# A gate and up pass with its instructions left in written order, fewer GpSimd subtractions and a separate ring for side work

## The chip, the core and the metric

The kernel runs on one core of a Trainium2 chip. The metric is the device time of one execution, in microseconds (us). TensorE is called PE, VectorE DVE, ScalarE ACT, GpSimd POOL, and SyncE SP; here SP issues nearly every transfer.

## What is computed

One decoder layer on a sequence of 2048 rows of width 1024: a mixer of four head groups, an output projection with its residual, and a gated feed-forward block. Only the feed-forward block is touched:

```python
x = x + mixed @ w_out[l]
gu = rms_norm(x, norm_ffn[l]) @ w_gate_up[l]
x = x + (jax.nn.silu(gu[..., :D_FF]) * gu[..., D_FF:]) @ w_down[l]
```

D_FF is 2816, everything is float32.

## The kernel before

**Stages.** A and B compute the mixer, C the output projection, D the gate and up product with the silu, E the down product. Stages A, C, D and E are written as plain loops, and the tile framework's scheduler decides at compile time, by a priority in written order and its own clock, in which order each engine gets its instructions. Stage B (L795) opens a region called `manual_schedule` for all five engines, in which each engine gets the region's instructions in the order in which they are written.

**Precision.** A float32 product is made of three passes: each operand is split into a rounded high part and the low remainder, and PE adds high*high, low*high and high*low (L1589 to L1591). Splitting an operand is one ACT copy and one subtraction (`split`, L1528 to L1532, for weights; L1373 and L1374 for x).

**Stage D.** The work is cut as a 2 by 2 block product with seven block products instead of eight. A unit is one (b, s, a): b is the half of the rows (0, 1), s one of 11 sets of 256 columns (`NSET`), a is gate (0) or up (1). The order is b, then s, then a: 44 units. A unit has seven products of 12 matmuls (four slices of the contraction, three passes), each against one of seven fixed combinations of x: A11, S2, S1, S3, A12, A22, S4. For one half b, all seven x combinations stay in SBUF, split; they are loaded from `xf_d` (L1369 to L1374, 512 KB an instruction, two for each combination). When b goes from 0 to 1 they are loaded anew during the last unit of b = 0.

In `gate_up` (L1577 on) each product is followed by its eviction from the PSUM bank (L1598, L1602, L1606, L1610, L1614, L1615, L1618, L1621) and then by `step`, which writes one piece of the next unit's weight preparation (`prep_gu`) and one piece of side work. Three banks are used twice within a unit: p1, p7 and p5 get a second product added after their first eviction. So the product T4, the sixth, can't start before L1610 has read p7 after the fourth. After an up unit eight DVE operations (L1627 to L1634) form the seven combinations `hs` of the hidden values, and one transfer stores them (L1717).

**Preparation.** `prep_gu` forms four combinations of the raw weights on DVE (L1540, L1541, L1546, L1551), using a scratch tile `tt`, and splits seven operands. Six of the low parts are made by POOL and one (T4) by DVE (L1531). Raw weights come two units ahead into a ring `raw` of four 4 KB buffers (L1524).

**Side work.** Three kinds, all in b = 0: `prep_tw` forms differences of the down weights (four POOL subtractions a set, L1568 to L1573), in up units; `last_rows` finishes the last two row tiles of the x combinations (ACT, PE transposes at L1655, POOL, SP) in the gate units of s = 1 and 2; and x loads (L1369). Their buffers come from the same ring `raw` and from the same scratch `tt` (its tile for the down weights is `ttd`) as the weight preparation; `last_rows` shares the buffer of `hs`.

**Stage E** (L1818 to L1820 are its matmuls) loads `araw` (hidden) and `braw` (down weights), splits both and runs seven products.

Of the kernel before, what the change touches and what calls it, by code (L numbers as in the profile page):

```python
# [21 lines left out]
NT = T // 128  # L22
# [150 lines left out]
def kernel(ctx, tc, x, norm_mix, w_in, lru_conv_w, lru_conv_b, lru_w_gates, lru_b_gates,  # L173
# [1334 lines left out]
    with ExitStack() as Dx:  # L1508
        rw = Dx.enter_context(tc.tile_pool(name="rw", bufs=1, reuse_waits="tile"))
        gw = Dx.enter_context(tc.tile_pool(name="gw", bufs=10, reuse_waits="tile"))  # L1510
        xdb = Dx.enter_context(tc.tile_pool(name="xdb", bufs=1, reuse_waits="tile"))
        hp = Dx.enter_context(tc.tile_pool(name="hp", bufs=2, reuse_waits="tile"))
        psg = Dx.enter_context(tc.tile_pool(name="psg", bufs=7, space=PSUM, reuse_waits="tile"))
        pst = Dx.enter_context(tc.tile_pool(name="pst3", bufs=1, space=PSUM, reuse_waits="tile"))

        def raw_tile(name):
            return rw.tile([128, 1024], F32, name=name, tag="raw", bufs=4)

        def load_gu(s, a):
            c0 = a * DFF + s * 256  # L1520
            raws = []
            for c in range(2):
                raw = raw_tile("guraw").rearrange("p (k c) -> p k c", k=HK)
                SP.dma_start(raw, wgu[c * 512:(c + 1) * 512, c0:c0 + 256].rearrange("(k p) c -> p k c", p=128))  # L1524
                raws.append(raw)
            return raws

        def split(src, sub):  # L1528
            g = [gw.tile([128, HK, 128], F32R, name=f"g{a}") for a in "hl"]
            ACT.copy(g[0], src)  # L1530
            sub.tensor_sub(g[1], src, f(g[0]))  # L1531
            return g  # L1532

        def prep_gu(raws, ws):


            b11, b12, b21, b22 = raws[0][:, :, :128], raws[0][:, :, 128:], raws[1][:, :, :128], raws[1][:, :, 128:]
            tt = rw.tile([128, 2, HK, 128], F32, name="tt", tag="tt", bufs=1)
# [12 lines left out]
            DVE.tensor_sub(b21, b21, tt[:, 1])  # L1551
            yield
            ws["T4"] = split(b21, DVE)
            yield
            ws["B22"] = split(b22, POOL)
            yield

        def prep_tw(k):

            raws = []  # L1560
            for c in range(2):
                raw = raw_tile("dnraw")
                SP.dma_start(raw, wdn[(2 * k + c) * 128:(2 * k + c + 1) * 128, :])
                raws.append(raw)
            yield
            b11, b12, b21, b22 = [r[:, n * 512:(n + 1) * 512] for r in raws for n in range(2)]
            tt = rw.tile([128, 2, 512], F32, name="ttd", tag="tt", bufs=1)
            POOL.tensor_sub(tt[:, 0], b12, b11)  # L1568
            POOL.tensor_sub(tt[:, 1], b22, tt[:, 0])
            SP.dma_start(tw_d[k][0:2].rearrange("i p c -> p i c"), tt)  # L1570
            yield
            POOL.tensor_sub(b12, b22, b12)
            POOL.tensor_sub(b21, b21, tt[:, 1])  # L1573
            SP.dma_start(tw_d[k][2], b12)
            SP.dma_start(tw_d[k][3], b21)
            yield

        def gate_up(x, ws, gate, step):

# [16 lines left out]
            p1 = bank()  # L1596
            product(p1, "B11", A11, True)
            ACT.copy(ev[:, 0], p1)  # L1598
            step(A11)
# [3 lines left out]
            step(S2)  # L1603
            p5 = bank()
            product(p5, "T1", S1, True)
            ACT.copy(ev[:, 3], p5)  # L1606
            step(S1)
# [3 lines left out]
            step(S3)  # L1611
# [4 lines left out]
            step(A12)  # L1616
            product(p7, "T4", A22, False)
            DVE.tensor_add(ev[:, 2], p7, ev[:, 1])  # L1618
            step(A22)
            product(p5, "B22", S4, False)  # L1620
            DVE.tensor_add(ev[:, 1], p5, ev[:, 1])  # L1621
            if gate is None:
                ACT.activation(ev[:, 1:], ev[:, 1:], AF.Silu)
                step(S4)
                return ev
            hs = hp.tile([128, 7, 512], F32, name="hs", tag="hs", bufs=1)
            DVE.tensor_mul(hs[:, A11], p1, gate[:, 0])  # L1627
            DVE.tensor_mul(hs[:, A12], gate[:, 1], ev[:, 1])
            DVE.tensor_mul(gate[:, 2], gate[:, 2], ev[:, 2])
            DVE.tensor_mul(hs[:, A22], gate[:, 3], ev[:, 3])  # L1630
            DVE.tensor_add(hs[:, S1], gate[:, 2], hs[:, A22])
            DVE.tensor_sub(hs[:, S2], hs[:, S1], hs[:, A11])
            DVE.tensor_sub(hs[:, S3], hs[:, A11], gate[:, 2])
            DVE.tensor_sub(hs[:, S4], hs[:, A12], hs[:, S2])  # L1634
            step(S4)
            return hs

        def last_rows(t):

            buf = hp.tile([128, 3, 1024], F32, name="rows", tag="hs", bufs=1)  # L1640
            xt, xo, y = [buf[:, i] for i in range(3)]
# [8 lines left out]
            xo, y, s = [b.rearrange("p (k t) -> p k t", t=128) for b in (xo, y, xt)]  # L1650
# [8 lines left out]
            to_factors(t, xo, y, s, POOL)  # L1659
            yield  # L1660

        preps, side = [], []

        def run(todo):
            while todo:
# [12 lines left out]
        for q in seq[:2]:  # L1678
            raws[q] = load_gu(*q[1:])
        gu[seq[0]] = {}  # L1680
        preps.append(prep_gu(raws.pop(seq[0]), gu[seq[0]]))
        drain(preps)
        x = dict(x0)
        for i in LATE:
            x[i] = x_tiles(xdb, i)
            side.append(x_factor(0, i, x[i], rw, "raw", 4))
        run(side)
        new = {}
        for n, q in enumerate(seq):
            b, s, a = q  # L1690
            last = b == 0 and s == NSET - 1 and a == 1

            def step(i):
                run(preps)
                run(side)
                if n == 0:
                    run(side)
# [10 lines left out]
            if b == 0 and a == 0:  # L1708
                if s in (1, 2):
                    side.append(last_rows(NT - 3 + s))  # L1710
            if b == 0 and a == 1:
                side.append(prep_tw(s))
            if a == 0:
                gate = gate_up(x, gu.pop(q), None, step)
            else:
                hs = gate_up(x, gu.pop(q), gate, step)
                SP.dma_start(hf_d[b][s].rearrange("i p t -> p i t"), hs)  # L1717
            drain(preps)
            drain(side)
            if last:  # L1720
                x = new


    with ExitStack() as Ex:
# [11 lines left out]
        def total(i):  # L1736
            return lambda k: tw_d[k][i]

        prods = [(A11, block(0, 0)), (A12, block(1, 0)), (S2, total(1)), (S1, total(0)), (S4, block(1, 1)),
                 (S3, total(2)), (A22, total(3))]  # L1740
# [131 lines left out]
```

## Time and profile before

| | |
|---|---|
| median of 3 runs | 2805.86 us (2801.77 to 2811.09) |
| profiled execution | 2809.3 us |
| its span | 2807.5 us |
| mean granted TensorE clock | 0.977 of full |
| PE busy | 2640.9 us (94%) |
| DVE, ACT, POOL busy | 1731.3 (62%), 1343.1 (48%), 1122.7 us (40%) |
| transfers | 364.69 MB, 130 GB/s mean |

The span runs from the first to the last instruction of the profiled execution; 1.8 us of its time lie outside. Stage D stands at about 1413 to 2381 us of the span, with b = 0 until about 1929; stage E follows. A timeline row gives start, duration, engine, line, output and inputs, and in brackets the idle time before it and what ended that.

### The profile page before, as it was taken

The numbers are of one execution on the slowest core, as the hardware profiler recorded it, in microseconds if no ns is written. First come the engines' busy times: TensorE is split into PE (matmuls) and PEld (weight loads), VectorE is DVE, ScalarE is ACT, GpSimd is POOL, SyncE is SP. The second block draws the span as 40 slices with busy tenths as digits, with TensorE's granted clock in tenths as the row PEclk, the third lists the DMA queues.
The fourth block names the chain that finished last, engine by engine and source line by source line (L and its number), as shares of the span: only waits on it lengthen the run. The fifth ranks groups of instructions, "written<-read, shape, count | busy, mean of one in ns | idle before, by whom it ended". The sixth has DMA issues, their size and how long they took to land.

```text
span 2807.5 us, 39068 instructions
## 1 busy us (share of the span) xinstructions
PE 2640.9 (94%) x13483; PEld 2226.4 (79%) x13483; DVE 1731.3 (62%) x3701; ACT 1343.1 (48%) x2863; POOL 1122.7 (40%) x1118
## 2 busy tenths in 40 slices
PE   7999898999998999999978989897999999999999
PEld 6899767889888888988866767675788887888887
DVE  6762686358899999877665555455655654333343
ACT  5431574169988888875533222223333333433331
POOL 1100125124565568812055545453444443422450
PEclk9999999999999999999999999998999999999999
DMA  5444314253423110068656443345333332864563
GB/s 162 127 109 114 118 49 150 71 167 100 107 70 83 39 54 24 16 225 252 227 167 198 134 144 126 135 145 174 114 105 110 109 105 76 273 199 135 172 192 120
DMA packets 298245, 364.69 MB, mean 130 GB/s; under 512 B 23024, under 2 KB 189119, under 8 KB 297279
## 3 DMA queue, kind: packets, MB, share of 16 engines
q1 hardware_dynamic: 295870, 358.01, 41.0%
q10 hardware_dynamic: 2176, 4.19, 0.4%
q8 instruction: 106, 1.74, 0.3%
q14 instruction: 93, 0.75, 0.1%
HBM read 240.24 MB, written 121.90 MB: 129 GB/s over the span
## 4 chain that ended last, share of the span: by engine, by line
PE 48%; DVE 5%; DMA 3%; issue 3%; POOL 2%; ACT 1%; SPq 0%; POOLq 0%; DVEq 0%; ACTq 0%
PE gu L1589 8%; PE gu L1591 8%; PE gu L1590 8%; PE d L1820 5%; PE d L1819 5%; PE d L1818 5%; POOL gl L1531 2%; PE obank L1137 2%; PE px L215 1%; PE px L217 1%; PE px L216 1%; PE tp L1115 1%; DMA xraw<-xf_d 1%; PE S L1045 1%; DMA dnraw<-in_w_down_dram 1%
## 5 line engine op out<-in xcount | busy, mean ns | idle before, releaser
L1589 PE MATMUL gu<-xh,gh 128*128 128x512 f32 x1232 | 498.2, 405 | 72.0 <-DVE gate L1610 46.9
L1591 PE MATMUL gu<-xl,gh 128*128 128x512 f32 x1232 | 494.3, 402 | 6.7 <-DVE xl L1374 6.6
L1590 PE MATMUL gu<-xh,gl 128*128 128x512 f32 x1232 | 492.5, 400 | 0.6 <-POOL gl L1531 0.6
L1531 POOL TENSOR_TENSOR gl<-guraw,gh 128x512 fp32r<-128x512 f32 x176 | 247.1, 1413 | 277.4 <-ACT gh L1530 277.3
L1589 PEld LDWEIGHTS gu<-xh,gh 128*128 128x128 f32 x1232 | 238.4, 193 | 132.8 <-DVE gate L1610 51.1
L1591 PEld LDWEIGHTS gu<-xl,gh 128*128 128x128 f32 x1232 | 237.6, 193 | 66.2 <-DVE xl L1374 11.0
L1752 DVE TENSOR_TENSOR al<-araw,ah 128x512 fp32r<-128x512 f32 x154 | 125.1, 815 | 258.2 <-ACT ah L1751 233.0
L1590 PEld LDWEIGHTS gu<-xh,gl 128*128 128x128 f32 x1232 | 238.6, 194 | 54.8 <-POOL gl L1531 1.1
L925 POOL TENSOR_TENSOR pl<-pf,ph 128x512 fp32r<-128x512 f32 x179 | 230.3, 1294 | 113.3 <-ACT ph L911 49.8
L1820 PE MATMUL d<-bh,al 128*128 128x512 f32 x616 | 240.0, 390 | 1.3 <-DVE al L1752 1.2
L1818 PE MATMUL d<-bh,ah 128*128 128x512 f32 x616 | 239.7, 389 | 0.6 <-ACT bh L1762 0.5
L1819 PE MATMUL d<-bl,ah 128*128 128x512 f32 x616 | 239.9, 389 | 0.2
L1082 ACT ACTIVATE P<-P,mn 128x1024 f32<-128x1024 f32 (+7 forms) x256 | 225.5, 888 | 21.5 <-DVE mn L1060 21.3
L1530 ACT CAST gh<-guraw 128x512 fp32r<-128x512 f32 x220 | 133.9, 620 | 197.9 <-PE gu L1591 93.4
L1751 ACT CAST ah<-araw 128x512 fp32r<-128x512 f32 x154 | 95.8, 624 | 265.3 <-PE d L1819 262.4
L1137 PE MATMUL obank<-ph,v 128*128 128x256 f32 (+1 forms) x744 | 197.5, 293 | 3.3 <-ACT ob L962 3.1
L1531 POOL TENSOR_TENSOR gl<-tt,gh 128x512 fp32r<-128x512 f32 x88 | 125.8, 1435 | 184.8 <-ACT gh L1530 158.6
L1115 PE MATMUL tp<-ident,P 128*128 128x128 f32 x1368 | 198.0, 276 | 1.2 <-DVE t L975 0.9
L1045 PE MATMUL S<-k,q 128*128 128x512 f32 (+2 forms) x432 | 175.4, 408 | 23.4 <-DVE mn L1060 19.2
L1763 POOL TENSOR_TENSOR bl<-braw,bh 128x512 fp32r<-128x512 f32 x77 | 108.9, 1424 | 203.6 <-ACT bh L1762 193.0
L1137 PE MATMUL obank<-pl,v 128*128 128x256 f32 (+1 forms) x744 | 185.7, 283 | 3.8 <-DVE pl L920 2.4
L1115 PEld LDWEIGHTS tp<-ident,P 128*128 128x128 f32 x1368 | 161.2, 142 | 12.6 <-DVE t L975 1.2
(505 smaller groups left out, 6307.6 us busy)
## 6 DMA issues: line engine op xcount, KB each, us to landing
guraw<-in_w_gate_up_dram SPq DMA_DIRECT2D x88, 512.0 KB
hf_d<-hs SPq DMA_DIRECT2D x22, 1792.0 KB
araw<-hf_d SPq DMA_DIRECT2D x154, 256.0 KB
q<-qk_d SPq DMA_DIRECT2D x80, 256.0 KB
xt<-in_x_dram SPq DMA_DIRECT2D x32, 512.0 KB
xraw<-xf_d SPq DMA_DIRECT2D x28, 512.0 KB
dnraw<-in_w_down_dram SPq DMA_DIRECT2D x22, 512.0 KB
braw<-tw_d SPq DMA_DIRECT2D x44, 256.0 KB
```

The costliest lines, as they stand in the source:

```text
L925: POOL.tensor_sub(tp["pl"], tp["pf"], f(tp["ph"]))
L1045: PE.matmul(dst, u["q"].tile[:, 0, qs], ks, start=True, stop=False)
L1082: ACT.activation(t, t, AF.Exp, bias=c["mn", a][:, n:n + 1], scale=-1.0, accum_out=c["sum"][:, x, a:a + 1])
L1115: PE.transpose(tp["tp"][:, si, a * 128:(a + 1) * 128], c["P", a, kt // 8][:, kt % 8 * 128:(kt % 8 + 1) * 128], ident)
L1137: PE.matmul(c["o"][:, cs], u["v"].tile[:, kt, :], tp[x][:, si, cs], start=gi == 0 and i == 0, stop=last and i == len(todo) - 1, skip_group ...
L1531: sub.tensor_sub(g[1], src, f(g[0]))
L1589: PE.matmul(p, wh, xh, start=first and k == 0, stop=False, skip_group_check=True)
L1590: PE.matmul(p, wl, xh, start=False, stop=False, skip_group_check=True)
L1591: PE.matmul(p, wh, xl, start=False, stop=k == HK - 1, skip_group_check=True)
L1818: PE.matmul(p, a[0][:, ts], w[0], start=first, stop=False, skip_group_check=True)
L1819: PE.matmul(p, a[0][:, ts], w[1], start=False, stop=False, skip_group_check=True)
L1820: PE.matmul(p, a[1][:, ts], w[0], start=False, stop=stop_, skip_group_check=True)
```

## The change

Stage D gets a `manual_schedule` region for all five engines, so what is written first is issued first on its engine. The order of writing stays eviction, then `step`, but the products T4 and B22 change places. The split of T2, T1 and T3 goes from POOL to DVE; four splits are then on DVE and three on POOL. High and low part of a weight are one tile. Side work gets its own ring `sd` (two buffers); the down weights' differences are done in place in halves of 256 columns, so eight POOL subtractions of half the size, a set later and in gate units; `last_rows` goes to the up units. The x loads use `sd` (two loads in flight) and give one of two subtractions to POOL. The gate, up and `last_rows` tiles share a ring of three buffers. The hidden products are made in place in the gate tile as the evictions come, and the four sums (`hidden`) and the stores are written into the next unit's steps.

```diff
-    LATE = (S3, A12, A22, S4)
+    LATE = (S3, A12, S4, A22)
...
+        sd = Dx.enter_context(tc.tile_pool(name="sd", bufs=2, reuse_waits="tile"))
-        hp = Dx.enter_context(tc.tile_pool(name="hp", bufs=2, reuse_waits="tile"))
+        hp = Dx.enter_context(tc.tile_pool(name="hp", bufs=3, reuse_waits="tile"))
...
+        Dx.enter_context(tc.manual_schedule(engines={mybir.EngineType.PE, mybir.EngineType.Activation,
+                                                     mybir.EngineType.DVE, mybir.EngineType.Pool,
+                                                     mybir.EngineType.SP}))
+        tts = [rw.tile([128, 2, HK, 128], F32, name="tt") for _ in range(1)]
...
-            ws["T2"] = split(tt[:, 1], POOL)
+            ws["T2"] = split(tt[:, 1], DVE)
             yield
-            ws["T1"] = split(tt[:, 0], POOL)
+            ws["T1"] = split(tt[:, 0], DVE)
+            yield
             DVE.tensor_sub(b12, b22, b12)
-            yield
-            ws["T3"] = split(b12, POOL)
+            ws["T3"] = split(b12, DVE)
             yield
             ws["B21"] = split(b21, POOL)
-            DVE.tensor_sub(b21, b21, tt[:, 1])
             yield
-            ws["T4"] = split(b21, DVE)
-            yield
+            DVE.tensor_sub(tt[:, 0], b21, tt[:, 1])
             ws["B22"] = split(b22, POOL)
             yield
+            ws["T4"] = split(tt[:, 0], DVE)
+            yield
...
         def prep_tw(k):
...
+            for n in range(2):
+                cs = slice(n * 256, n * 256 + 256)
+                raw = sd.tile([128, 2, 2, 256], F32, name="dnraw", tag="side")
...
+                yield
+                b11, b12, b21, b22 = raw[:, 0, 0], raw[:, 0, 1], raw[:, 1, 0], raw[:, 1, 1]
+                POOL.tensor_sub(b11, b12, b11)
+                POOL.tensor_sub(b12, b22, b12)
+                yield
+                POOL.tensor_sub(b22, b22, b11)
+                POOL.tensor_sub(b21, b21, b22)
+                yield
+                SP.dma_start(tw_d[k][:, :, cs].rearrange("i p c -> p i c"), raw.rearrange("p c n i -> p (c n) i"))
+
+        def x_parts(half, i, x):
+            parts = []
+            for k in (0, 2):
+                raw = sd.tile([128, 2, 512], F32, name="xraw", tag="side")
+                SP.dma_start(raw, xf_d[half][i, k:k + 2].rearrange("k p t -> p k t"))
+                parts.append(raw)
             yield
+            for k, raw, sub in zip((0, 2), parts, (DVE, POOL)):
+                ACT.copy(x[0][:, k:k + 2], raw)
+                sub.tensor_sub(x[1][:, k:k + 2], raw, f(x[0][:, k:k + 2]))
             yield
...
             product(p1, "B21", A12, False)
             if gate is None:
                 ACT.activation(ev[:, 0], p1, AF.Silu)
+            else:
+                DVE.tensor_mul(gate[:, 0], p1, gate[:, 0])
             DVE.tensor_add(ev[:, 3], ev[:, 2], ev[:, 3])
+            if gate is not None:
+                DVE.tensor_mul(gate[:, 3], gate[:, 3], ev[:, 3])
+            step(4)
+            product(p5, "B22", S4, False)
+            DVE.tensor_add(ev[:, 2], p5, ev[:, 1])
...
             product(p7, "T4", A22, False)
-            DVE.tensor_add(ev[:, 2], p7, ev[:, 1])
+            DVE.tensor_add(ev[:, 1], p7, ev[:, 1])
...
+        def hidden(b, s, h, t):
+            yield
+            DVE.tensor_add(t[:, 0], h[:, 1], h[:, 3])
+            DVE.tensor_sub(t[:, 1], t[:, 0], h[:, 0])
+            yield
+            DVE.tensor_sub(t[:, 2], h[:, 0], h[:, 1])
+            DVE.tensor_sub(t[:, 3], h[:, 2], t[:, 1])
+            yield
+            yield
+            to = hf_d[b][s]
+            SP.dma_start(to[A11], h[:, 0])
+            SP.dma_start(to[A12:A22 + 1].rearrange("i p t -> p i t"), h[:, 2:4])
+            SP.dma_start(to[S1:S4 + 1].rearrange("i p t -> p i t"), t)
+            yield
...
-            def step(i):
+            def step(j):
+                run(sums)
                 run(preps)
                 run(side)
                 if n == 0:
-                    run(side)
+                    run(late)
+                    run(late)
                 if last:
+                    i = (A11, S2, S1, S3, A12, S4, A22)[j]
                     new[i] = x_tiles(xda if i in EARLY else xdb, i)
-                    for _ in x_factor(1, i, new[i], rw, "raw", 4):
+                    for _ in x_parts(1, i, new[i]):
                         pass
```

## Rows read from the trace of the kernel before

**Rows 1.** Windows: b = 0, change of b, b = 1. PE, PEld, DVE, ACT, POOL; PEclk, DMA, GB/s.

```profile
1498.86:1911.88 413.02, 368.93 (x1521) 296.26 (x1520) 226.66 (x257) 117.43 (x194) 214.93 (x151) 0.95 0.43 140
1911.88:2055.07 143.19, 125.38 (x505) 98.56 (x504) 84.93 (x98) 51.38 (x75) 57.98 (x40) 0.93 0.47 149
2055.07:2364.19 309.12, 309.12 (x1345) 252.17 (x1344) 171.00 (x221) 99.18 (x158) 133.02 (x93) 1.00 0.31 101
```

**Rows 2.** Timeline of ACT: first eviction of a unit (L1598).

```profile
1425.31 0.59 ACT L1598 COPY gate<-gu 128x512 f32<-128x512 f32 x1 [1.69 <-PE gu L1591]
1443.33 0.59 ACT L1598 COPY up<-gu 128x512 f32<-128x512 f32 x1 [0.94 <-PE gu L1591]
...
1498.86 0.59 ACT L1598 COPY up<-gu 128x512 f32<-128x512 f32 x1 [0.59 <-PE gu L1591]
...
1911.88 0.59 ACT L1598 COPY up<-gu 128x512 f32<-128x512 f32 x1 [0.59 <-PE gu L1591]
...
2055.07 0.59 ACT L1598 COPY up<-gu 128x512 f32<-128x512 f32 x1 [0.59 <-PE gu L1591]
...
2364.19 0.59 ACT L1598 COPY up<-gu 128x512 f32<-128x512 f32 x1 [0.59 <-PE gu L1591]
```

**Rows 3.** Waits of PE from 1500 to 1900: total us, times, longest.

```profile
PE gu L1589 <- DVE gate L1610: 38.9, 8, 6.6
```

**Rows 4.** Timeline of DVE ahead of one such wait.

```profile
1622.70 0.69 DVE L1551 TENSOR_TENSOR guraw<-guraw,tt 128x512 f32<-128x512 f32 x1 [4.34 <-POOL gl L1531]
...
1624.76 1.76 DVE L1546 TENSOR_TENSOR guraw<-guraw 128x512 f32<-128x512 f32 x1
1626.44 1.75 DVE L1531 TENSOR_TENSOR gl<-guraw,gh 128x512 fp32r<-128x512 f32 x1
1628.11 0.68 DVE L1610 TENSOR_TENSOR gate<-gu,gate 128x512 f32<-128x512 f32 x1
```

**Rows 5.** Groups by shape, DVE, 1500 to 1900: busy us, mean ns, idle before.

```profile
L1546 DVE TENSOR_TENSOR guraw<-guraw 128x512 f32<-128x512 f32 x18 | 21.9, 1218 | 0.0
L1633 DVE TENSOR_TENSOR hs<-hs,gate 128x512 f32<-128x512 f32 x9 | 16.0, 1782 | 0.0
...
L1541 DVE TENSOR_TENSOR tt<-guraw,tt 128x512 f32<-128x512 f32 x18 | 12.3, 686 | 0.3
...
L1621 DVE TENSOR_TENSOR up<-gu,up 128x512 f32<-128x512 f32 x9 | 6.1, 678 | 0.0
```

**Rows 6.** The same, DVE, 2055 to 2345 (b = 1).

```profile
L1632 DVE TENSOR_TENSOR hs<-hs 128x512 f32<-128x512 f32 x8 | 14.2, 1774 | 0.0
...
L1546 DVE TENSOR_TENSOR guraw<-guraw 128x512 f32<-128x512 f32 x15 | 10.3, 684 | 0.0
```

**Rows 7.** The same, POOL and ACT, 1500 to 1900.

```profile
L1531 POOL TENSOR_TENSOR gl<-guraw,gh 128x512 fp32r<-128x512 f32 x72 | 100.2, 1403 | 59.6 <-ACT gh L1530 59.6
...
L1572 POOL TENSOR_TENSOR dnraw<-dnraw 128x512 f32<-128x512 f32 x9 | 15.7, 1744 | 0.0
...
L1530 ACT CAST gh<-guraw 128x512 fp32r<-128x512 f32 x89 | 53.5, 620 | 84.2 <-DVE guraw L1551 37.4 <-PE gu L1591 31.8 <-POOL gl L1531 12.2
```

**Rows 8.** Chain of work: four transposes of last_rows; an x load and its copy.

```profile
1491.89 0.85 PE tpl L1655 x4
...
1945.27 3.81 DMA xraw<-xf_d
1949.10 1.05 ACT xh L1373
```

**Rows 9.** Timeline of SP inside stage B: loads of stages C and B.

```profile
877.94 1.72 SPq L1427 DMA_DIRECT2D mh<-m_d  x1
...
892.92 109.36 SPq L880 DMA_DIRECT2D q<-qk_d  x21
```

**Rows 10.** Windows of PE alone at the start of stage E.

```profile
2380.00:2385.00 5.00, 4.29 (x15) 1.00 0.01 3
2385.00:2390.00 5.00, 3.77 (x16) 1.00 0.18 70
```

More of the change, by code (lines that the diff above doesn't have):

```diff
@@ L1528, in split @@
         def split(src, sub):
[L1529 to L1532, printed above, removed]
+            g = gw.tile([128, 2, HK, 128], F32R, name="g")
+            ACT.copy(g[:, 0], src)
+            sub.tensor_sub(g[:, 1], src, f(g[:, 0]))
+            return g[:, 0], g[:, 1]
         def prep_gu(raws, ws):
             b11, b12, b21, b22 = raws[0][:, :, :128], raws[0][:, :, 128:], raws[1][:, :, :128], raws[1][:, :, 128:]
-            tt = rw.tile([128, 2, HK, 128], F32, name="tt", tag="tt", bufs=1)
+            tt = tts[0]
             ws["B11"] = split(b11, POOL)
@@ L1567, in prep_tw @@
[L1567 to L1575, printed above, removed]
+            for n in range(2):
+                cs = slice(n * 256, n * 256 + 256)
+                raw = sd.tile([128, 2, 2, 256], F32, name="dnraw", tag="side")
+                for c in range(2):
+                    SP.dma_start(raw[:, c], wdn[(2 * k + c) * 128:(2 * k + c + 1) * 128, :].rearrange(
+                        "p (n c) -> p n c", n=2)[:, :, cs])
+                yield
[7 more added lines that the diff above has]
+                SP.dma_start(tw_d[k][:, :, cs].rearrange("i p c -> p i c"), raw.rearrange("p c n i -> p (c n) i"))
@@ L1598, in gate_up @@
             ACT.copy(ev[:, 0], p1)
-            step(A11)
+            step(0)
             p6 = bank()
@@ L1602, in gate_up @@
             DVE.tensor_add(ev[:, 1], p6, ev[:, 0])
-            step(S2)
+            step(1)
             p5 = bank()
@@ L1606, in gate_up @@
             ACT.copy(ev[:, 3], p5)
-            step(S1)
+            step(2)
             p7 = bank()
@@ L1614, in gate_up @@
                 ACT.activation(ev[:, 0], p1, AF.Silu)
+            else:
+                DVE.tensor_mul(gate[:, 0], p1, gate[:, 0])
             DVE.tensor_add(ev[:, 3], ev[:, 2], ev[:, 3])
-            step(A12)
+            if gate is not None:
[3 more added lines that the diff above has]
+            DVE.tensor_add(ev[:, 2], p5, ev[:, 1])
+            if gate is None:
+                ACT.activation(ev[:, 2:], ev[:, 2:], AF.Silu)
+            else:
+                DVE.tensor_mul(gate[:, 2], gate[:, 2], ev[:, 2])
@@ L1617, in gate_up @@
+            step(5)
             product(p7, "T4", A22, False)
-            DVE.tensor_add(ev[:, 2], p7, ev[:, 1])
-            step(A22)
-            product(p5, "B22", S4, False)
-            DVE.tensor_add(ev[:, 1], p5, ev[:, 1])
+            DVE.tensor_add(ev[:, 1], p7, ev[:, 1])
             if gate is None:
[L1623 to L1635, printed above, removed]
@@ L1636, in gate_up @@
-            return hs
+                ACT.activation(ev[:, 1], ev[:, 1], AF.Silu)
+            else:
+                DVE.tensor_mul(gate[:, 1], gate[:, 1], ev[:, 1])
+            step(6)
+            return ev
+        def hidden(b, s, h, t):
[12 more added lines that the diff above has]
+            yield
@@ L1638, in last_rows @@
         def last_rows(t):
-            buf = hp.tile([128, 3, 1024], F32, name="rows", tag="hs", bufs=1)
-            xt, xo, y = [buf[:, i] for i in range(3)]
+            buf = hp.tile([128, 2, 1024], F32, name="rows", tag="ev")
+            xt, xo = buf[:, 0], buf[:, 1]
             SP.dma_start(xt, x1_d[t * 128:(t + 1) * 128, :])
@@ L1658, in last_rows @@
                 yield
-            to_factors(t, xo, y, s, POOL)
+            to_factors(t, xo, sd.tile([128, KD, 128], F32, name="xy", tag="side"), s, POOL)
             yield
-        preps, side = [], []
         def run(todo):
@@ L1680 @@
         gu[seq[0]] = {}
-        preps.append(prep_gu(raws.pop(seq[0]), gu[seq[0]]))
+        preps, side, late, sums = [prep_gu(raws.pop(seq[0]), gu[seq[0]])], [], [], []
         drain(preps)
@@ L1685 @@
             x[i] = x_tiles(xdb, i)
-            side.append(x_factor(0, i, x[i], rw, "raw", 4))
-        run(side)
+            late.append(x_parts(0, i, x[i]))
+        run(late)
+        run(late)
         new = {}
@@ L1707 @@
                 preps.append(prep_gu(raws.pop(seq[n + 1]), gu[seq[n + 1]]))
[L1708 to L1712, printed above, removed]
+            if b == 0 and a == 1 and s in (1, 2):
+                side.append(last_rows(NT - 3 + s))
+            if b == 0 and a == 0 and s:
+                side.append(prep_tw(s - 1))
+            if b == 1 and a == 0 and s == 2:
+                side.append(prep_tw(NSET - 1))
             if a == 0:
@@ L1715 @@
             else:
-                hs = gate_up(x, gu.pop(q), gate, step)
-                SP.dma_start(hf_d[b][s].rearrange("i p t -> p i t"), hs)
+                sums.append(hidden(b, s, gate, gate_up(x, gu.pop(q), gate, step)))
             drain(preps)
             drain(side)
+            drain(late)
             if last:
                 x = new
+        drain(sums)
     with ExitStack() as Ex:
```

21 lines of the change are left out of this document (7 added, 14 removed).

## The prediction

> **What bounds the kernel now.** I read the page first: PE is busy in nearly all of the span, so the question is where it isn't at full rate. The windows give that by stage. With b = 1 PE is busy for all of 309.12 us at full clock. With b = 0 it is busy for 368.93 of 413.02 us at a mean clock of 0.95 [rows 1]. The same work, then, is done at two rates. The first eviction of each up unit is a clean mark for them: eight sets with b = 1 take 2364.19 - 2055.07 = 309.12 us, 38.64 each; nine sets with b = 0 take 1911.88 - 1498.86 = 413.02 us, 45.89 each [rows 2]. The difference over nine sets is 413.02 - 9 x 38.64 = **65.3 us**. Of it 44.1 us are idle PE and the rest is the half-speed clock after each stop.
>
> The waits name the cause: between 1500 and 1900 us PE stood eight times, 38.9 us in all, for the DVE eviction L1610 [rows 3]. The timeline of DVE shows why it was late. DVE had nothing to do for 4.34 us because L1551 waits for a POOL subtraction, then did three preparations, two of them in 1.75 us each, and only then the eviction, which takes 0.68 us [rows 4]. So the stop is one of order: the eviction stands behind preparation which waits for POOL, and POOL has the side work's subtractions in between, in buffers that it shares with the preparation.
>
> **The change, part by part.**
>
> *The order, with b = 0.* One set has 2 x 84 matmuls; at full rate it is 38.64 us [rows 2]. Afterwards the eviction of p7 is written ahead of the preparation of its step, and with T4 and B22 exchanged PE needs p7 only after two more products, 2 x 38.64 / 14 = 5.5 us later, not one. What lies ahead of it on DVE at most is the rest of earlier steps. I count DVE by set after the change: 9 evictions that read PSUM, and 25 operations with both inputs in SBUF (16 of preparation, 4 sums, 3 products, 2 additions). The first kind takes 0.68 us; the second 0.69, or up to 1.78 when it meets POOL, with a mean of 1.22 in one group that often does [rows 5]. POOL has 6 weight subtractions of 1.40 us a set, and 8 of half width for the down weights, which no row shows; half of 1.40 to 1.74 is 0.70 to 0.87, and I take 0.8 [rows 7]: 14.8 us. Before, POOL had 12 + 4 full ones, 12 x 1.40 + 4 x 1.7 = 24 us. DVE comes to 9 x 0.68 + 25 x 0.9 = 29 us (0.9 lies between 0.69 and 1.22, as POOL does less than it did), against 38.64 us. ACT has 14 copies of 0.62 us for the splits [rows 7] and ten evictions, half its time. So neither PE's helpers nor POOL is full over a set, and I give back the whole 65.3 us, less two things. The eight transposes of each `last_rows` now stand in the PE order as fixed, 4 x 0.85 = 3.4 us for both [rows 8], and the norm of the last tile, a chain of a square, a square root and a few small DVE operations that PE's transposes then wait for, may hold PE for 3 us (an estimate: its two wide ACT passes by the 1.05 us row, a third for the rest [rows 8]). **-59 us**; bounds -65 and -45, the latter if each gate unit (below) still stops for 1.5 us with as much again lost to clock.
>
> *Half b = 1.* PE is already at full rate with DVE's preparation at 0.68 and only some sums at 1.77 us [rows 1, 6]. POOL goes from 12 to 6 subtractions a set, DVE from 28 to 34 operations. Cover is 38.64 us for about 28: 0.
>
> *The first unit.* Four x combinations go through two buffers. One takes a load of 3.81 us, an ACT copy of 1.05 [rows 8] and a POOL subtraction of twice the width of the 1.40 us row [rows 7]: 7.7 us, so four need 31 us and some 5 us of lead, and the strictly ordered first unit takes about 36 us where a full rate one takes 19.3: 17 lost. Before, the first unit cost 1443.33 - 1425.31 = 18.0, but the next two 55.5 instead of 38.6 [rows 2], 17 lost as well. **0**, bounds -8 and +8.
>
> *The change of b.* Before, this costs 143.19 - 3 x 38.64 = 27.3 us [rows 1]. Afterwards seven combinations pass through the same two buffers, 7.7 us each. The first is there about 12 us after the last unit of b = 0 starts (its load is issued early, its copy waits for the first product), the seventh 6 x 7.7 = 46 us later, at 58. The load, the copy and the subtraction are written into that unit's steps, so what is queued behind a copy that waits for its transfer is ACT's next eviction: the first of the next unit stands behind the last copy, at 58 - 2.8 = 55 us. The fifth product needs that bank, so three products of 2.76 us follow at 56, and the two units end at 64 and not at 38.6. That is 25.5 lost, plus about 4 for a slow clock after 20 us of stop: 29.5. **+2**, bounds -8 and +12.
>
> *SP.* It gets everything in written order too: the loads of weights two units ahead, the down weights, the stores. A store that waits for POOL now holds the next loads, but a weight load has a whole unit of 19.3 us. `hidden`'s stores are written in step 4; the first tile of them is needed by the next up unit, 8 us and a first product later. With the ring of three this is covered; the tile behind a `last_rows` waits for its stores until about 6 us into the gate unit, and PE needs it at 11. 0.
>
> *Stage E.* If its loads had to follow all of stage D's stores, PE would start late. In stage B, which has the same kind of region, SP issued stage C's load L1427 at 877.94 us, ahead of B's own load at 892.92 [rows 9]: later code can go in between. So I keep the present start, which loses 2 x 5 us of windows with 15 and 16 matmuls instead of 23, 3 us [rows 10]. **+1**, bounds -2 and +15.
>
> Sum: -59 + 0 + 0 + 2 + 0 + 1 = -56 us. The profiled execution took 2809.3 us (span 2807.5, 1.8 around it), 3.4 above the median of 2805.86; from the median the sum gives **2750 us**. Its own range adds the near bounds: 2732 to 2774.
>
> **A rule against it.** The rows show that a DVE operation with a PSUM input stays at 0.68 us while those with two SBUF inputs reach 1.78 [rows 5]. The change moves three splits of exactly the second kind to DVE in each unit. Priced as if DVE and POOL were one resource, a gate unit with side work needs 13 x 0.69 + 3 x 1.40 + 8 x 0.8 = 19.6 us of 19.3, its up unit 12 x 0.69 + 3 x 1.40 = 12.5; the set 32 of 38.6, and before 19 x 0.69 + 24 = 37 of 45.9. So the set fits and the gate unit only just fails, and what it is late the up unit takes up.
>
> The Trainium skill, SBUF — State Buffer, section "Who interferes with whom", says that a DVE instruction with two SBUF inputs and a GpSimd instruction that reads SBUF exclude one another, the one that comes second waiting in full. By that rule the gate unit of the paragraph above is the tightest place, and the first rival's time results.
>
> **The rivals.**
>
> *The gate unit falls behind (chance 0.2).* By the count above, 19.6 us plus waits between ACT and DVE, nine gate units with b = 0 stop for about 2.5 us, with half as much again lost to clock: 9 x 3.5 = +32, so **2782**. For it: 19.6 of 19.3. Against: PE needs p7 5.5 us after its product, and most of POOL's side work is written after that point.
>
> *DVE becomes the bound (0.06), the slower end.* If every operation with two SBUF inputs costs the 1.78 us of the worst group [rows 5], a set needs 25 x 1.78 + 9 x 0.68 = 50.6 us. Nine sets with b = 0 lose 4.7 us each and ten with b = 1 lose 12: +162, **2968**. It decides from a set of (9 x 45.89 + 10 x 38.64) / 19 = 42.1 us, a mean of 1.44 us. For it: three groups lie near 1.6 to 1.8. Against: others lie at 0.69 in the same stretch, and POOL works less.
>
> *Stage E starts after D's stores (0.1).* Idle from the last product through four sums, the stores and the first loads, 15 us: **2765**. Against it [rows 9].
>
> *It does nothing (0.04).* If POOL's rate and not order set the 45.9 us a set, the stop would move on: **2806**. Against: POOL is busy 214.93 of 413.02 us [rows 1].
>
> **How the numbers follow.** My forecast has 0.6. A measurement of this kernel can tell about 0.3%, 8.4 us, from no change. Forecast, first and third rival end faster: 0.90; no change 0.04; slower 0.06. The range takes the forecast's lower bound and reaches past the first rival with a little for a costlier first unit: 2730 to 2788.
>
> **What would show it.** Right: sets of about 38.6 us with b = 0 and a clock of 1.0; PE's wait for L1610's successor gone; the change of b near 29 us with PE waiting for ACT; POOL near 15 us a set. Wrong: DVE busy over 36 us a set, evictions of p7 more than 5 us after their product, PE idle at the start of stage E for over 5 us, or PE idle in every gate unit with side work.

## The result and the profile after

The changed kernel takes **2762.39 us** (median of 4 runs, 2760.96 to 2763.34); beside it the kernel before took 2806.37 us (4 runs). The ratio is 0.9843, with a 95% interval of 0.9826 to 0.986: 44.0 us less. The forecast was 2750 us in a range of 2730 to 2788. The profiled execution has a span of 2760.9 us, 46.6 less than before, and a mean granted clock of 0.981 of full.

The windows of the changed kernel between the same marks (first eviction of an up unit, now L1612), with the columns of [rows 1]: the nine sets with b = 0, six of these alone, the change of b, and b = 1.

```profile
1493.42:1855.21 361.79, 352.05 (x1529) 286.64 (x1528) 241.98 (x312) 121.31 (x213) 148.79 (x134) 0.99 0.50 164
1623.37:1855.21 231.84, 231.84 (x1009) 189.12 (x1008) 154.60 (x205) 73.74 (x127) 90.08 (x84) 1.00 0.47 157
1855.21:2002.86 147.65, 121.92 (x505) 98.19 (x504) 91.17 (x110) 50.63 (x77) 49.23 (x33) 0.90 0.45 144
2002.86:2311.98 309.12, 309.12 (x1345) 252.16 (x1344) 190.06 (x273) 98.30 (x168) 65.69 (x48) 1.00 0.31 101
```

Against [rows 1] the nine sets shrank from 413.02 to 361.79 us, b = 1 is unchanged to the hundredth, and the change of b grew from 143.19 to 147.65. In the second row PE is busy for all of 231.84 us at clock 1.00: six sets of 38.64 us, with side work in each.

The timeline of ACT shows the marks, as in [rows 2]; the third and fourth follow the two up units with `last_rows`.

```profile
1455.23 0.58 ACT L1612 COPY up<-gu 128x512 f32<-128x512 f32 x1
1493.42 0.59 ACT L1612 COPY up<-gu 128x512 f32<-128x512 f32 x1 [0.94 <-PE gu L1605]
1535.64 0.59 ACT L1612 COPY up<-gu 128x512 f32<-128x512 f32 x1 [1.59 <-DMA hf_d<-gate]
1584.82 0.59 ACT L1612 COPY up<-gu 128x512 f32<-128x512 f32 x1 [1.03 <-DMA hf_d<-gate]
...
1855.21 0.59 ACT L1612 COPY up<-gu 128x512 f32<-128x512 f32 x1 [0.94 <-PE gu L1605]
...
1911.04 0.58 ACT L1612 COPY gate<-gu 128x512 f32<-128x512 f32 x1
```

By these marks the 46.6 us are -5.4 from the start to the mark at 1493.42 (1498.86 before), -51.2 in the nine sets, +4.5 at the change of b, 0 with b = 1, and +5.6 in the rest (2760.9 - 2311.98 = 448.9, against 2807.5 - 2364.19 = 443.3). Two of the nine sets took 42.2 and 49.2 us; the other seven average 270.39 / 7 = 38.63.

The waits of PE in the same pass, 1400 to 2400 us (total us, times, longest):

```profile
PE gu L1603 <- ACT gate L1612: 18.2, 1, 18.2
PE tpl L1684 <- ACT rows L1677: 9.7, 2, 8.4
PE gu L1603 <- ACT g L1532: 8.0, 1, 8.0
PE gu L1603 <- ACT up L1620: 7.5, 1, 7.5
PE d L1851 <- ACT bh L1795: 4.4, 1, 4.4
PE gu L1603 <- ACT gate L1620: 4.2, 1, 4.2
...
PE d L1852 <- POOL bl L1796: 2.5, 1, 2.5
```

The wait of [rows 3] (p7's eviction by DVE, now L1624) is gone. What is left is mostly ACT: 8.0 and 4.2 us in the first set (the 8.0 us were there before too), 9.7 us for the norm of `last_rows` (L1677), 18.2 and 7.5 us at the change of b, and 4.4 + 2.5 us at the start of stage E.

The groups of DVE by shape, 1623 to 1855 us, and then those of POOL (busy us, mean ns, idle before), which answer to [rows 5, 7]:

```profile
L1533 DVE TENSOR_TENSOR g<-tt,g 128x512 fp32r<-128x512 f32 x37 | 31.6, 854 | 24.0 <-ACT g L1532 24.0
L1633 DVE TENSOR_TENSOR gate<-gate,up 128x512 f32<-128x512 f32 x6 | 10.0, 1664 | 0.2
...
L1640 DVE TENSOR_TENSOR gate<-gate,up 128x512 f32<-128x512 f32 x6 | 4.2, 692 | 0.2
...
L1624 DVE TENSOR_TENSOR up<-gu,up 128x512 f32<-128x512 f32 x6 | 4.2, 692 | 5.6 <-PE gu L1605 5.6
```

```profile
L1573 POOL TENSOR_TENSOR dnraw<-dnraw 128x256 f32<-128x256 f32 x12 | 10.9, 908 | 0.5
...
L1570 POOL TENSOR_TENSOR dnraw<-dnraw 128x256 f32<-128x256 f32 x12 | 8.9, 740 | 0.0
```

The collision is still there: one product with two inputs in SBUF (L1633) takes 1664 ns, another of the same form (L1640) 692, like the eviction with an input in PSUM. In the set from 1623.37 us L1633 starts at 1636.20 us, while POOL is busy (1634.33 to 1637.32), and L1640 at 1638.50, when POOL is idle. But DVE is busy 154.60 / 6 = 25.8 us of a set, POOL 90.08 / 6 = 15.0, and PE does not notice.

### The profile page after: what moved, and what is told of

Its sections match the earlier page's. It is cut to its first block, busy times and chain, and to the rows that moved or that the text cites. A ratio compares the mean times of both kernels' runs of the same rounds, so it can differ in the third digit from the quotient of the medians.

```text
span 2760.9 us, 39168 instructions
## 1 busy us (share of the span) xinstructions
PE 2618.3 (95%) x13483; PEld 2214.5 (80%) x13483; DVE 1762.6 (64%) x3822; ACT 1340.3 (49%) x2885; POOL 966.8 (35%) x1041
## 5 line engine op out<-in xcount | busy, mean ns | idle before, releaser
L1603 PE MATMUL gu<-xh,g 128*128 128x512 f32 x1232 | 490.3, 398 | 39.2 <-ACT gate L1612 18.2
L1605 PE MATMUL gu<-xl,g 128*128 128x512 f32 x1232 | 487.4, 396 | 3.9 <-POOL xl L1588 3.4
L1604 PE MATMUL gu<-xh,g 128*128 128x512 f32 x1232 | 487.2, 395 | 0.5 <-POOL g L1533 0.5
L1533 POOL TENSOR_TENSOR g<-guraw,g 128x512 fp32r<-128x512 f32 x132 | 185.5, 1412 | 543.0 <-ACT g L1532 542.4
L1603 PEld LDWEIGHTS gu<-xh,g 128*128 128x128 f32 x1232 | 234.1, 190 | 94.4 <-ACT gate L1612 18.6
L1785 DVE TENSOR_TENSOR al<-araw,ah 128x512 fp32r<-128x512 f32 x154 | 116.1, 754 | 273.8 <-ACT ah L1784 247.5
L1605 PEld LDWEIGHTS gu<-xl,g 128*128 128x128 f32 x1232 | 234.1, 190 | 59.3 <-POOL xl L1588 4.3
L1604 PEld LDWEIGHTS gu<-xh,g 128*128 128x128 f32 x1232 | 234.3, 190 | 53.5 <-POOL g L1533 1.1
L1082 ACT ACTIVATE P<-P,mn 128x1024 f32<-128x1024 f32 (+7 forms) x256 | 225.6, 889 | 19.8 <-DVE mn L1060 19.6
L1532 ACT CAST g<-guraw 128x512 fp32r<-128x512 f32 x176 | 105.0, 617 | 141.5 <-DVE guraw L1549 126.6
L1533 DVE TENSOR_TENSOR g<-tt,g 128x512 fp32r<-128x512 f32 x132 | 112.5, 853 | 86.7 <-ACT g L1532 85.8
```

Source lines behind the costliest of these rows:

```text
L1082: ACT.activation(t, t, AF.Exp, bias=c["mn", a][:, n:n + 1], scale=-1.0, accum_out=c["sum"][:, x, a:a + 1])
L1533: sub.tensor_sub(g[:, 1], src, f(g[:, 0]))
L1603: PE.matmul(p, wh, xh, start=first and k == 0, stop=False, skip_group_check=True)
L1604: PE.matmul(p, wl, xh, start=False, stop=False, skip_group_check=True)
L1605: PE.matmul(p, wh, xl, start=False, stop=k == HK - 1, skip_group_check=True)
```

## The experiments

All times are medians, with ratios to the kernel before that ran beside them (2805 to 2808 us); where two intervals overlap, the two kernels can hardly be told apart. The parts are read from one profile of each kernel, which can lie some us from its median (e4's is 2750.62 us). "Ten sets" runs from the up mark of s = 0 to that of s = 10 with b = 0; at full rate it is 386.4 us. "Change" is the next three sets, "end" the time from the last mark to the span's end. From the marks of each profile (us; b = 1 is 309.12 in all of them):

| kernel | median | ratio (95%) | first mark | ten sets | change | end |
|---|---|---|---|---|---|---|
| before | 2806.37 | 1 | 1443.33 | 468.55 | 143.19 | 443.3 |
| after | 2762.39 | 0.9843 (0.9826 to 0.986) | 1455.23 | 399.98 | 147.65 | 448.9 |
| e1_no_order | 2753.04 | 0.9815 (0.9799 to 0.9831) | 1444.94 | 418.04 | 129.69 | 448.5 |
| e2_pool_splits | 2769.49 | 0.9872 (0.9853 to 0.9892) | 1454.66 | 404.61 | 146.69 | 449.2 |
| e3_old_products | 2757.8 | 0.9828 (0.981 to 0.9846) | 1459.72 | 396.20 | 148.06 | 441.9 |
| e4_four_side | 2744.16 | 0.9778 (0.9759 to 0.9798) | 1453.75 | 403.24 | 133.83 | 449.0 |
| n1_free_pool | 2777.11 | 0.9891 (0.9874 to 0.9907) | 1449.62 | 438.53 | 129.06 | 449.3 |
| n2_free_products | 2763.04 | 0.9843 (0.9828 to 0.9857) | 1456.25 | 423.77 | 127.60 | 443.7 |
| n3_free_both | 2786.33 | 0.9924 (0.9909 to 0.9938) | 1451.49 | 446.31 | 134.58 | 443.4 |
| n4_before_ring | 2759.71 | 0.9832 (0.9817 to 0.9847) | 1455.51 | 427.92 | 123.14 | 443.1 |
| n5_in_place_only | 2775.74 | 0.9896 (0.9882 to 0.9909) | 1439.50 | 436.17 | 145.24 | 443.6 |
| n6_ring_only | 2769.75 | 0.987 (0.9857 to 0.9884) | 1451.41 | 423.05 | 141.92 | 443.5 |
| b1_order_plus | 2735.53 | 0.9748 (0.9735 to 0.9762) | 1450.92 | 395.27 | 133.23 | 442.2 |
| b2_free_plus | 2753.51 | 0.9814 (0.9801 to 0.9828) | 1449.03 | 416.78 | 128.05 | 449.2 |

### One part of the change taken back

**The fixed order.** The region is left out of the changed kernel, all else stays.

```diff
-        Dx.enter_context(tc.manual_schedule(engines={mybir.EngineType.PE, mybir.EngineType.Activation,
-                                                     mybir.EngineType.DVE, mybir.EngineType.Pool,
-                                                     mybir.EngineType.SP}))
```

> The changed kernel without its region of fixed order; rings, engines and product order stay. Theory (the order did it): without it the evictions stand behind preparation again, sets with b = 0 go back from 38.6 to 44 us or more, time 2790 to 2810 us. Rival (the separate ring and POOL's lighter load did it): sets stay near 38.6 us, 2755 to 2770 us.

2753.04 us, 9 us below the changed kernel; the intervals of the two ratios just overlap, so what is sure is that it is not slower. The table shows a trade: the fixed order saves 418.04 - 399.98 = 18.1 us in the ten sets, loses 147.65 - 129.69 = 18.0 at the change of b and 10.3 before the first mark (4.1 of them stand ahead of the first eviction of stage D, at 1425.31 against 1421.19 us; behind it, PE's 4.2 us for ACT's L1620, in the waits above, have no counterpart in e1). The theory that the fixed order as a whole makes the gain falls.

**The engine split.** The low parts of T2, T1 and T3 go back to POOL.

```diff
-            ws["T2"] = split(tt[:, 1], DVE)
+            ws["T2"] = split(tt[:, 1], POOL)
...
```

> The changed kernel with the low parts of T2, T1 and T3 made by POOL again. Theory (order): POOL has 12 x 1.41 + 8 x 0.8 = 23 us a set of 38.6 and a unit's lead, so sets stay at 38.6 us and the time within 2755 to 2770 us. Rival (the move from POOL to DVE did it): POOL's share holds DVE up as before, sets with b = 0 over 42 us, 2790 us or more.

2769.49 us, and the sets without `last_rows` stay at 38.6 us, as the theory has it. In the fixed order the split is worth 7 us (0.3%, hardly clear of the noise), none of it in those sets.

**The products.** T4 goes ahead of B22 again, in the order of preparation and of the x loads too.

```diff
-            product(p5, "B22", S4, False)
+            product(p7, "T4", A22, False)
...
-            product(p7, "T4", A22, False)
+            product(p5, "B22", S4, False)
```

> The changed kernel with T4 ahead of B22 again, so that PE needs p7 one product after its first product and not two. Theory (order alone is enough): DVE starts that eviction within 0.3 us of the product and takes 0.7, against 2.76 us, so sets stay at 38.6 us, 2755 to 2770 us. Rival (the longer lead did it): PE waits for it in most units with side work, 2780 us or more.

2757.8 us, not to be told from the changed kernel, sets of 38.6 us: the theory again. With two products of lead on p7 or with one, PE does not wait: the exchange buys nothing while the order is fixed. The end is 7 us shorter (below).

**The side ring.** Four side buffers and eight weight buffers.

```diff
-        gw = Dx.enter_context(tc.tile_pool(name="gw", bufs=10, reuse_waits="tile"))
-        sd = Dx.enter_context(tc.tile_pool(name="sd", bufs=2, reuse_waits="tile"))
+        gw = Dx.enter_context(tc.tile_pool(name="gw", bufs=8, reuse_waits="tile"))
+        sd = Dx.enter_context(tc.tile_pool(name="sd", bufs=4, reuse_waits="tile"))
```

> The changed kernel with four buffers for side work instead of two (and 8 weight buffers instead of 10, to make room). Theory (the change of b costs 31.7 us because two buffers let seven x combinations through at 7.7 us each and ACT's next eviction stands behind them): with four, about 4.5 us each, so the change of b loses 8 to 14 us, the first unit 3 to 5 us less, 2730 to 2748 us. Rival (the transfers' own rate sets it): 2755 to 2765 us.

2744.16 us, within the forecast: the change of b loses 133.83 - 115.92 = 17.9 us in place of 31.7, though more than the 8 to 14 expected. The timeline of ACT shows why, first in the changed kernel (x copies L1587, then the eviction behind the last of them):

```profile
1902.23 1.04 ACT L1587 CAST xh<-xraw 128x1024 fp32r<-128x1024 f32 x1 [4.63 <-DMA xraw<-xf_d]
1904.01 1.05 ACT L1587 CAST xh<-xraw 128x1024 fp32r<-128x1024 f32 x1 [0.22 <-DMA xraw<-xf_d]
1910.09 1.04 ACT L1587 CAST xh<-xraw 128x1024 fp32r<-128x1024 f32 x1 [5.03 <-DMA xraw<-xf_d]
1911.04 0.58 ACT L1612 COPY gate<-gu 128x512 f32<-128x512 f32 x1
```

and with four buffers:

```profile
1894.53 1.99 ACT L1587 CAST xh<-xraw 128x1024 fp32r<-128x1024 f32 x2
1896.42 0.58 ACT L1612 COPY gate<-gu 128x512 f32<-128x512 f32 x1
```

The eviction L1612 starts as the last x copy ends; with two buffers that copy waited 5.03 us for its transfer. The eviction comes 1911.04 - 1855.21 = 55.8 us after the mark with two buffers and 1896.42 - 1856.99 = 39.4 us with four, and PE's wait for L1612 falls from 18.2 to 6.4 us.

### The same parts without the fixed order

The kernel without the region, with the low parts of T2, T1 and T3 on POOL (n1), with T4 ahead of B22 (n2), and with both (n3); the edits are those of e2 and e3.

> No fixed order, and T2, T1, T3 split by POOL again (own ring and new product order stay). Theory ring (what freed the sets is that side work has its own buffers): sets with b = 0 mostly near 38.6 us, 2750 to 2770 us. Theory POOL (without a fixed order it takes the lighter POOL): sets over 42 us, 2780 us or more.

> No fixed order, and T4 ahead of B22 again (own ring and the DVE splits stay). Theory ring: sets mostly near 38.6 us, 2750 to 2770 us. Theory lead (without a fixed order it takes the two products of lead on p7): PE waits for that eviction again, sets over 42 us, 2780 us or more.

> No fixed order, POOL splits and the old product order; left of the change are the rings, the down weights' halves in place and the hidden sums in the next unit. Theory ring: 2750 to 2775 us. Theories POOL and lead together: sets back at 44 to 46 us, 2790 to 2806 us.

2777.11, 2763.04 and 2786.33 us. Only n2 falls into the time of its theory ring; n1 and n3 lie between the times of their theories. In all three most sets that carry side work take 40 to 60 us and later ones 38.6, which none of the theories foresaw. Against e1's 2753.04 us the three cost 24, 10 and 33 us; within the fixed order the first two cost 7 and -5. The waits of PE in n3, 1540 to 1705 us, show it stopped by p7's eviction again (L1621 there):

```profile
PE gu L1600 <- DVE gate L1621: 22.3, 3, 12.6
```

In the same stretch DVE waits 59.1 us for POOL in n3 and 63.9 in n1 (at L1551, a preparation). In e2, which is n1 with the fixed order, the waits of DVE from 1627 to 1859 us have none for POOL. So split and exchange shield PE from late evictions, and here that is needed only where the scheduler chooses the order.

### The side work's buffers alone

**Own ring and no shared scratch.** The kernel before, with the scheduler's order, the old engine split and products; only the side work gets two buffers of its own, and the down weights' differences are made in place. One weight buffer of ten is given up for the room.

```diff
-                raw = raw_tile("dnraw")
+                raw = sd.tile([128, 1024], F32, name="dnraw", tag="side")
...
-            tt = rw.tile([128, 2, 512], F32, name="ttd", tag="tt", bufs=1)
-            POOL.tensor_sub(tt[:, 0], b12, b11)
-            POOL.tensor_sub(tt[:, 1], b22, tt[:, 0])
+            POOL.tensor_sub(b11, b12, b11)
             POOL.tensor_sub(b12, b22, b12)
...
-            side.append(x_factor(0, i, x[i], rw, "raw", 4))
+            side.append(x_factor(0, i, x[i], sd, "side", 2))
...
-                    for _ in x_factor(1, i, new[i], rw, "raw", 4):
+                    for _ in x_factor(1, i, new[i], sd, "side", 2):
```

> The kernel before with one part of the change: side work (down weights, x loads) in a ring of two buffers of its own, the down weights' differences in place so that they no longer use the scratch of the preparation (9 weight buffers of each kind instead of 10, to make room). Theory ring: sets with b = 0 fall from 45.9 to under 41 us, 2755 to 2780 us. Rival (the ring alone is not it): sets stay over 44 us, 2790 to 2815 us.

2759.71 us: this alone gives what the whole change gives. Its windows tell how (1500 to 1650 us, then 1700 to 1860):

```profile
1500.00:1650.00 150.00, 129.10 (x541) 102.80 (x541) 76.37 (x91) 48.34 (x85) 106.11 (x78) 0.94 0.69 229
1700.00:1860.00 160.00, 160.00 (x698) 130.56 (x697) 86.81 (x120) 51.73 (x82) 68.63 (x50) 1.00 0.31 101
```

and the groups of POOL in the second stretch, which are all there are:

```profile
L1532 POOL TENSOR_TENSOR gl<-guraw,gh 128x512 fp32r<-128x512 f32 x34 | 46.8, 1377 | 61.6 <-ACT gh L1531 61.6
L1532 POOL TENSOR_TENSOR gl<-tt,gh 128x512 fp32r<-128x512 f32 x16 | 22.0, 1373 | 32.1 <-ACT gh L1531 32.1
```

No down weight is prepared there any more. Freed from the weights' ring and scratch, the scheduler ran the side work ahead: the last of it is at 1629 us, not at 1929 as before. The first sets carry it and take 51.2, 52.5, 45.1 and 46.6 us, and PE waits for p7's eviction (now L1611) there, from 1450 to 1650 us, in gate and in up units:

```profile
PE gu L1590 <- DVE up L1611: 14.8, 4, 5.9
PE gu L1590 <- DVE gate L1611: 13.6, 3, 6.3
```

In this stretch DVE's L1552, two places ahead of that eviction in a gate unit, waits 61.8 us for POOL, up to 11.3 at a time. From 1650.87 us on a set takes 38.6. So n4 does not hide the side work, it does it in fewer sets. e1 does the same (last down weights of this batch in 1600 to 1700 us, sets of 40 to 51 us until 1669.07).

**One of the two.** n5 keeps the shared ring and only drops the scratch; n6 has the ring and keeps the scratch `ttd`.

> The kernel before with the down weights' differences in place, so that they no longer take the scratch tile of the preparation; the ring of raw buffers stays shared (9 weight buffers of each kind). Theory ring (the shared raw buffers made the preparation late): sets with b = 0 stay at 44 us or more, 2785 us or more. Theory scratch (the shared scratch tile did): sets fall to 38.6 us, 2755 to 2770 us.

> The kernel before with side work's own ring of two buffers, but the down weights' differences still in the scratch tile of the preparation (9 weight buffers of each kind). Theory ring: sets with b = 0 fall to 38.6 us, 2755 to 2775 us. Theory scratch: sets stay at 44 us or more, 2785 us or more.

2775.74 and 2769.75 us. Both theories miss: the sets do not stay and do not fall to 38.6, whichever sharing goes. In both kernels a set's worth of side work stays in each set, as before, and a steady set takes 41.1 us (n5) or 40.3 (n6), against 45.2 before and 38.64 in the changed kernel. The waits of PE from 1700 to 1860 us, in n5 and then in n6:

```profile
PE gu L1589 <- DVE gate L1610: 7.2, 4, 1.9
```

```profile
PE gu L1590 <- DVE gate L1611: 5.6, 4, 1.4
```

In the kernel before the same four waits are 18.2 us. So either sharing, taken away alone, removes 4.1 to 4.9 of the 6.6 us a set, with no order fixed; 1.7 to 2.5 remain. The timeline of DVE shows what became of the stop of [rows 4], here in n5:

```profile
1782.81 0.69 DVE L1551 TENSOR_TENSOR guraw<-guraw,tt 128x512 f32<-128x512 f32 x1 [3.70 <-POOL gl L1531]
1783.53 0.69 DVE L1540 TENSOR_TENSOR tt<-guraw 128x512 f32<-128x512 f32 x1
1784.14 0.68 DVE L1610 TENSOR_TENSOR gate<-gu,gate 128x512 f32<-128x512 f32 x1
```

DVE still waits for POOL, but the eviction starts 1.33 us after the start of L1551. In the kernel before it starts 1628.11 - 1622.70 = 5.41 us after it, as L1541, L1546 and L1531 stand ahead of it as well; 5.4 us in nine of the ten gate units with b = 0 and s from 1 on, 1.3 us in all ten of n5 and in all ten of n6. What either edit removed is thus three preparations ahead of the eviction in the scheduler's order, some 4.1 us, and not DVE's waiting for POOL: from 1700 to 1860 us that is 21.2 us before and 32.9 us in n5 and in n6.

Only the kernels with a fixed order have full rate with side work in every set. That it is the order which hides the last 1.7 to 2.5 us is not shown by itself: these kernels differ from n5 and n6 also in that both sharings are gone and that T4's combination goes to the scratch (`tt[:, 0]`) and no longer over the operand whose low part POOL is making, an edit that no run takes back. Without the order that edit is not enough, as n1 and n3 have it. The number of weight buffers (9 for 10) was not tried alone, nor a fixed order with the shared ring.

### A better version

The fixed order with four side buffers and eight weight buffers; the tile of `last_rows` loaded ahead of the weights, with its norm a step earlier against its transposes; and in the last set the four sums stored ahead of the blocks.

```diff
+            if b == 1 and s == NSET - 1:
+                SP.dma_start(to[S1:S4 + 1].rearrange("i p t -> p i t"), t)
             SP.dma_start(to[A11], h[:, 0])
             SP.dma_start(to[A12:A22 + 1].rearrange("i p t -> p i t"), h[:, 2:4])
...
+            if b == 0 and a == 1 and s in (1, 2):
+                side.append(last_rows(NT - 3 + s))
+                run(side)
             if n + 2 < len(seq):
```

> The changed kernel with four side buffers, the row tile of last_rows loaded ahead of the unit's weights and normed one step earlier, and the last set's sums stored ahead of its products so that stage E's loads can pass. Four buffers gave 18 us; the two sets with last_rows lose 14 us more than a full rate set and should lose 4; stage E starts 5.6 us later than before and should lose 1 to 3 of it: 2725 to 2738 us. If these waits hide others: 2740 us or more.

2735.53 us (5 runs), within the forecast and the fastest of all, 27 us under the changed kernel. The parts: change of b 133.23 us, as in e4; end 442.2, 6.8 less than e4's; the two sets with `last_rows` 44.1 us each. The nine sets lose 358.39 - 347.76 = 10.6 us over full rate in place of 14.0, so this part gave 3 us and not the forecast 10.

**Four buffers without the order.** e1 with the buffers of e4.

> No fixed order, with four side buffers and 8 weight buffers. Without a fixed order the change of b already costs 18 us less than with it, so the four buffers give less here: 2740 to 2755 us. If two buffers hold it up all the same: 2735 us or less.

2753.51 us, as forecast and as e1. At the change of b the four buffers give 129.69 - 128.05 = 1.6 us here and 13.8 with the order fixed, where ACT's eviction is queued behind the x copies.

## Why the prediction was right, and where it was wrong

**The nine sets, -59: measured -51.2.** The mechanism held in its outcome: sets of 38.6 us, clock 1.00, the wait for p7's eviction gone, POOL at 15.0 us a set (forecast 14.8), half-width subtractions of 740 to 908 ns (forecast 800), DVE at 25.8 us (forecast 29). The step "the stop is one of order" stands: in n5 and n6 the stop shrinks with the three preparations that leave DVE's queue ahead of the eviction, while DVE waits for POOL as before (five preparations stood there, with two that [rows 4] leaves out, where the prediction counted three). What it missed is that the order need not be written by hand: the scheduler itself chooses a better one once either buffer is no longer shared. So the time alone does not speak for the region, as e1 without it and n4 with the buffers alone took about as long; what the region does is to keep side work in every set at full rate, where e1 and n4 do it in a few slow ones. The exchange of T4 and B22, which the prediction counted on for 5.5 us of lead, is not needed for it (e3).

**`last_rows`, 3.4 + 3: measured 14.0.** This is the term that was mis-sized. PE stood 9.7 us for the norm, where 3 were forecast, and the clock was 0.90 in the second of the two sets. The prediction left out the transfer, and priced the norm's own chain too low. In the strict order of SP the load of the tile stands behind a store that waits for POOL and behind two weight loads:

```profile
1538.26 0.36 SPq L1576 DMA_DIRECT2D tw_d<-dnraw  x1
1538.67 1.59 SPq L1526 DMA_DIRECT2D guraw<-in_w_gate_up_dram  x2
1540.35 0.64 SPq L1671 DMA_DIRECT2D rows<-x_d  x1
```

That timeline of SP is of the changed kernel; ACT's first pass over the tile starts at 1546.47 us, after 5.22 us of waiting for it. PE's stop of 8.4 us runs from 1542.87 to 1551.30 us, so 3.6 us of it are the late tile. The other 4.8 are the norm's chain, with a load of ACT's function table that the forecast had not counted:

```profile
1547.64 1.28 ACT L240 ACT_TABLE_LOAD   x1
```

In b1, where the tile's load goes ahead of the weights, PE still waits 6.5 us: 1.6 for the tile (ACT starts at 1537.51 us) and 4.8 for the chain. "SP: 0" holds for the weights and fails here.

**The first unit, 0: measured -5.4**, within its bounds.

**The change of b, +2: measured +4.5.** The mechanism is as forecast, ACT's eviction behind the last x copy: 55.8 us after the mark (forecast 55), x copies paced by 7.5 us on average (second copies of the seven combinations from 1864.98 to 1910.09 us; forecast 7.7), 31.7 us lost (forecast 29.5). What the prediction missed is the comparison: with the new buffers and no fixed order the same place loses 129.69 - 115.92 = 13.8 us, so the order costs 18 us there.

**Stage E, +1: measured +5.6.** Later code can pass, as [rows 9] suggested: six loads of stage E (L1779, from 2311.80 us) are issued ahead of stage D's last stores. But the store of the two finished blocks (L1663) is now a transfer of its own, and the loads of the down weights stand behind it:

```profile
2327.22 0.37 SPq L1663 DMA_DIRECT2D hf_d<-gate  x1
2327.69 3.75 SPq L1790 DMA_DIRECT2D braw<-in_w_down_dram  x7
2334.03 0.38 SPq L1664 DMA_DIRECT2D hf_d<-up  x1
```

Before, five of them went ahead of the store (from 2372.54 us, the store at 2388.16). It is not the fixed order: e1 without it has an end of 448.5 us too. All six kernels with the exchanged products and this order of stores end in 448.5 to 449.3 us, all seven with the old products in 441.9 to 443.7, and b1, exchanged but with the sums stored first, in 442.2. Pair by pair (e3 against the changed kernel, n2 against e1, n3 against n1) the exchange costs 7.0, 4.8 and 5.9 us here; the prediction did not price that. In e3 L1663 is a transfer of its own too, but three of the loads are issued ahead of it:

```profile
2325.32 2.39 SPq L1790 DMA_DIRECT2D braw<-in_w_down_dram  x3
2332.73 0.38 SPq L1663 DMA_DIRECT2D hf_d<-gate  x1
```

There PE waits 1.7 us in all for the first operands of stage E, and 6.9 us (4.4 + 2.5) in the changed kernel. In b1, with the exchange, all seven loads are issued ahead of the three stores, from 2294.14 us on. By these rows it is the place of the loads in SP's queue that moves the end, and the exchange acts through it.

**The rivals.** The gate unit did not fall behind: PE has no idle time in six sets, though the count gave 19.6 us of exclusive work in 19.3. Collisions are rarer than that rival took them to be: DVE's splits of `tt` (T2, T1 and T4) average 854 ns, and T3's, which the rows above leave out, 693, nearer to 0.69 than to 1.78 us. The Trainium skill (SBUF — State Buffer, "Who interferes with whom") lets the one that comes second wait. The trace agrees that operations with two inputs in SBUF are the ones that grow (1664 against 692 ns above). No eviction came too late for it in the six sets. DVE did not become the bound (25.8 us a set), and stage E did not wait for all of D's stores.

**The sum.** -51.2 - 5.4 + 4.5 + 5.6 = -46.5 against -56: right in sign, 9 us too hopeful. `last_rows`, stage E and the change of b were 7.6, 4.6 and 2.5 us dearer than forecast; that the sum is not further off is luck, for the first unit gave 5.4 us where the forecast had 0.

## What to carry to other kernels

Before fixing an order, read what stands ahead of the late instruction in its engine's queue, and look for a ring or a scratch tile that side work and main work share: undoing that alone changed the scheduler's order and was worth the whole change here. In these runs the fixed order hid small work spread evenly, and cost time where a burst of transfers was written into it, since each copy that waited for its transfer held the evictions behind it: give such a burst more buffers. Price every load and store in the new queue order, those of rare steps too: a late load was all of one term missed here (stage E) and part of another (`last_rows`).

## What was not expected of the hardware and its schedule

- Two shared resources do not add up: 6.6 us a set together, but 4.1 and 4.9 us come back when either one goes, as either alone changes the order that the scheduler chooses.
- A decoupled side job is not hidden but gathered: n4's POOL is busy 106.11 of 150 us early and PE's clock falls to 0.94, and then PE is at full rate for all of the 160 us from 1700.
- The order in SP's queue of stage D's last stores and stage E's first loads moved the end of the kernel by 5 to 7 us, though the bytes are the same.
